# Moving four taps of a depthwise convolution from TensorE to VectorE and ScalarE in a transformer block

## The chip, the core and the metric

The kernel runs on one core of one Trainium2 chip. The time of a run is the device time of that core in microseconds (us). Five engines have instruction queues of their own: TensorE (PE in the profile, its weight loads PEld), VectorE (DVE), ScalarE (ACT), GpSimd (POOL) and SyncE (SP), which here only issues DMAs. Each runs its queue strictly in order, and semaphores order them against each other.

## The reference

One block, 256 tokens of width 1024: attention with eight heads beside a depthwise convolution, a projection, and a gated feed-forward part. Cut to what matters:

```python
u = rms_norm(h, mix_norm_g)
q, k, v, glu_a, glu_g = split(u @ w_in)            # 5 x 512 columns
attn_out = attention(heads(q), heads(k), heads(v), rel_bias)
# convolution, 512 channels, 31 causal taps for each channel
c = glu_a * sigmoid(glu_g)
c = depthwise_conv(c, conv_w) + conv_b
c = (c - mean(c)) * rsqrt(var(c) + 1e-5) * conv_ln_g + conv_ln_b
conv_out = silu(c)
h = h + concat(attn_out, conv_out) @ w_out
u = rms_norm(h, ffn_norm_g)
h = h + (silu(u @ w_gate) * (u @ w_up)) @ w_down   # width 2816
out = rms_norm(h, final_norm_g)
```

With 256 tokens there is one attention block, so it is plain causal softmax attention with a bias by distance.

## The kernel before

All data are float32. A product of two matrices is made of three: each operand is split into an upper part, rounded to the format that TensorE takes in one pass (`wh`, `uh`), and a lower part, the rest (`wl`, `ul`); the products are wh x uh, wh x ul, wl x uh. ScalarE makes a weight's upper part by a copy (step `h`), VectorE the lower part by a subtraction (step `w`, which also makes the upper part if `h` has not). Weights come in pairs of 512 KB tiles from HBM into six raw buffers (step `ld`, on SP's queue); a buffer comes free when its lower part has been made. SP issues in program order, and each load waits for the semaphore of the one eight places before it.

The order of the first part is written out by hand. `PROGRAM` is a table of steps; `ops` maps each name to a function and they are called in that order, so each engine's queue is the order of the table cut to its own instructions. The names that matter here:

- `a0.k`, `a1.i`: projection to the two halves of glu_a and glu_g; half 0 and half 1 are 256 channels each, in two chunks of 128. `sq`: squares of x on ScalarE, summed on VectorE in `accx`. `rs`: `rstd`, the scaling of the first norm: two matmuls `ps_x`, VectorE's `ms_x`, GpSimd's power `rc_x`, VectorE's two diagonals `dg_x`. `rb`: a matmul `pb_x` with the diagonals spreads the scaling over all partitions.
- `glu.half`: sigmoid and products into `upad`, padded by 30 columns. `ud`, `us`: `upad` goes through HBM into `ustk`, where one partition block of 32 holds one of four shifts.
- `cw.half` (`conv_weights`): VectorE makes `wstk`, the diagonal blocks of the convolution's weights, 32 columns for each of 48 instructions, out of `pv`. `pv` holds small columns; the late ones (taps, weights, an identity) come by `pl`, one DMA of 78 KB on SP's queue.
- `c.half.j` (`conv`): TensorE does four taps at a time, in `Q` = 6 quads: 24 taps, 24 matmuls of 128 x 32 by 256 for each chunk, into `pc`. `ct.half.lo.hi` (`conv_taps`): VectorE does the `ONV` = 7 others, one instruction for a tap and chunk, added up in `cacc`; tap 0 is a `tensor_scalar` with the bias. `co.half`: adds `pc` to `cacc`.
- `qk`, `qo`, `sc`, `t`, `n`, `fl`, `fo`: for a pair of heads hp, q and k, their scaling by `rb`, scores, logits and exponentials, division by the sum (`normed`), transposes, copies. `v`, `vt`, `pv`, `mo`: values, their scaling, the product with the probabilities, and the split of the result into `mh` and `ml`.
- `l.1` to `l.7` (`norm`): the convolution's norm over channels: mean by a matmul `pm` (2), subtraction, squares (6), sums (3), `rstd` (7), the matmul `pb_ln` (4), and in 5 the scaling of `cacc`, Silu, and the split into `mh` and `ml`, for four chunks. `o.k`: projection w_out for one chunk k of eight; `f.m`: its last three chunks for output block m, and the sum with x.

Behind the table comes the feed-forward part: eleven groups, each of gate and up products (`pf`) and the down product (`pd`) of an earlier group, then the last norm. There a third call of `rstd` also made two diagonals, which nothing reads.

[...]

Of the kernel before, what the change touches and what calls it, by code (L numbers as in the profile page):

```python
# [23 lines left out]
CC = 4  # L24
# [16 lines left out]
MIX = 48  # L41

PROGRAM = """
ld.a1_0 a0.0 a0.1 a0.2 a0.3 ld.a1_1 a0.4 a0.5 a0.6 hb pz a0.7 pl ld.qk0
w.a1_0.0 w.a1_0.1 zs zd sq.0 sq.1 w.a1_0.2 w.a1_0.3 sq.2 sq.3 sq.4 ld.qk1 a1.0 w.a1_1.0 sq.5 sq.6 sq.7 h.a1_1.1 h.qk0.0 h.qk0.1 a1.1 rs
w.a1_1.1 w.qk0.0 bd ld.qk2 a1.2 rb glu.0 ud.0 w.qk0.1 ld.v0 us.0 a1.3 w.qk1.0 w.qk1.1 glu.1 ud.1 ld.qk3 us.1
qk.0.0 qk.0.1 qo.0 h.qk2.0 h.qk2.1 w.qk2.0 w.qk2.1 cw.0 qk.1.0 ct.0.0.1 ld.v1 qk.1.1 qo.1 h.v0.0 h.v0.1 ct.0.1.3 qk.2.0 sc.0 sc.1 t.0 t.1
c.0.0 ct.0.3.4 h.qk3.0 w.v0.0 n.0 n.1 c.0.1 w.v0.1 h.qk3.1 w.qk3.0 ct.0.4.5 ct.0.5.7 qk.2.1 qo.2 ld.o0 fl.0 fo.0 fl.1 fo.1 w.qk3.1 co.0 h.v1.0 cw.1 w.v1.0
v.0 ld.o1 qk.3.0 h.v1.1 w.v1.1 h.o0.0 ct.1.0.2 qk.3.1 qo.3 h.o0.1 w.o0.0 ct.1.2.3 v.1 sc.2 sc.3 t.2 t.3 ld.o2
c.1.0 ct.1.3.4 n.2 n.3 c.1.1 ct.1.4.6 ct.1.6.7 h.o1.0 co.1 l.1 v.2 w.o0.1 v.3 fl.2 fl.3 vt fo.2 fo.3 l.2 ld.o3 w.o1.0  # L50
pv.0 mo.0 pv.1 mo.1 l.6 pv.2 mo.2 pv.3 mo.3 l.3 w.o1.1 ld.g0 w.o2.0 w.o2.1 ld.u0 o.0 o.1 l.7 w.o3.0 o.2 w.o3.1 ld.g1 l.4 l.5 w.g0.0 o.3 w.g0.1 o.4
# [10 lines left out]
def block_kernel(ctx, tc, xT, w_in, w_out, w_gu, w_down, pvec, gfin, relb, hot, out):  # L62
# [24 lines left out]
    act, vec, pool, sync = (InOrder(e) for e in (nc.scalar, nc.vector, nc.gpsimd, nc.sync))  # L87
# [92 lines left out]
    us = const.tile([P, KD * 2 * S + SHIFT], F32R, name="us")  # L180
# [3 lines left out]
    pv = const.tile([P, PV_N + 8], F32, name="pv")  # L184
# [3 lines left out]
    warm = const.tile([P, 1], F32, name="warm")  # L188
    accx = w1.tile([P, S], F32, name="accx")
# [5 lines left out]
    wstk = [w1.tile([P, 8 * Q, 32], F32, name=f"wstk{i}", tag="wstk", bufs=2) for i in range(2)]  # L195
# [23 lines left out]
    zs = w1.tile([H, ZN], F32, name="zs", tag="lg", bufs=2)  # L219
# [5 lines left out]
    col = lambda lo, i: pv[:, lo + i : lo + i + 1]  # L225


    def conv_weights(half):
        fold, cw = pv[:, PV_FOLD:PV_N], pv[:, PV_CW + half * 8 * Q :]
        vec.tensor_tensor(  # L230
            wstk[half],
            bass.AP(tensor=fold.tensor, offset=fold.offset, ap=[fold.ap[0], [0, 8 * Q], [1, 32]]),
            bass.AP(tensor=cw.tensor, offset=cw.offset, ap=[cw.ap[0], [1, 8 * Q], [0, 32]]), op=ALU.mult)

    def rstd(acc, n, eps, name, b):
        ps = bank(b, f"ps_{name}")
        for t in range(2):
            mm(ps[:, t : t + 1], acc[:, t * P : (t + 1) * P], ones[:, 0:1], start=True, stop=True)  # L240
# [310 lines left out]
    def a0(k):  # L551
# [284 lines left out]
```

## Time and profile before

| | us |
|---|---|
| median of 3 runs (294.02 to 294.55) | 294.12 |
| the profiled execution | 294.47 |
| its span, first to last instruction | 292.6 |
| TensorE busy in the span | 285.2 (97%) |
| VectorE | 201.9 (69%) |
| ScalarE | 151.7 (52%) |
| GpSimd | 42.8 (15%) |

The granted TensorE clock is 0.995 of full speed in the mean. A busy TensorE is not TensorE at its peak: the ends of its matmuls are modelled, and they overlap, so the distance from start to start is what counts. In the timelines, rows of the same form in a row are merged, with their number behind an x, and the duration is from the first start to the last end. An idle time in brackets is that of the engine just before the row, with what ended it.

### The profile page before, as it was taken

How to read it: one execution, taken by the hardware profiler on the slowest of the kernel's cores; microseconds unless marked ns; L12 is line 12 of the kernel's file. 1: busy time of each engine (PE TensorE's matmuls, PEld its weight loads, DVE VectorE, ACT ScalarE, POOL GpSimd, SP SyncE). 2: the span in 40 equal slices, each digit the busy share in tenths (PEclk: the TensorE clock that was granted, in tenths of full speed). 3: DMA queues.
4: the chain of work that ended last, by engine and by line, in shares of the span. 5: the costliest groups of instructions: out<-in, count | busy, mean ns of one | idle time of the engine just before them, and what ended most of it. 6: DMA issues, size and time to landing. Idle time of an engine off the chain costs nothing.

```text
span 292.6 us, 4768 instructions
## 1 busy us (share of the span) xinstructions
PE 285.2 (97%) x1749; PEld 244.7 (84%) x1749; DVE 201.9 (69%) x371; ACT 151.7 (52%) x260; POOL 42.8 (15%) x80
## 2 busy tenths in 40 slices
PE   8999999999999999999999999999999999999991
PEld 8999996986899998888888888888888888888881
DVE  3987999988897788967937557381738366321884
ACT  3885548908393678537717263361718173402531
POOL 2000100000000000143121313321401313130000
PEclk9999999999999999999999999999999999999998
DMA  7999699951138435999996949879794949420012
GB/s 216 339 391 335 239 292 240 386 163 63 66 95 283 156 123 202 272 329 290 355 273 170 305 129 325 300 227 369 239 281 155 299 120 328 143 72 0 0 59 87
DMA packets 22090, 63.74 MB, mean 218 GB/s; under 512 B 3178, under 2 KB 5938, under 8 KB 22066
## 3 DMA queue, kind: packets, MB, share of 16 engines
q1 hardware_dynamic: 18754, 54.94, 56.8%
q0 software_dynamic: 2880, 7.95, 10.1%
q10 hardware_dynamic: 432, 0.54, 0.5%
q8 instruction: 14, 0.23, 0.3%
q14 instruction: 10, 0.08, 0.1%
HBM read 58.10 MB, written 5.32 MB: 217 GB/s over the span
## 4 chain that ended last, share of the span: by engine, by line
PE 92%; issue 2%; DVE 2%; DMA 1%; SPq 1%; ACT 0%; POOLq 0%; POOL 0%; DVEq 0%
PE pf L74 41%; PE pd L74 18%; PE py L74 8%; PE pqk L74 8%; PE pv L74 4%; PE pc L74 4%; PE pa L74 3%; PE pg L74 3%; DMA raw_a<-in_w_in 1%; PE pt L77 1%; PE ps L74 1%; PE po L74 1%; DVE ht L85 1%; SPq L85 1%; DVE hg L85 0%
## 5 line engine op out<-in xcount | busy, mean ns | idle before, releaser
L74 PE MATMUL pf<-wl,us 128*128 128x512 f32 x176 | 68.5, 389 | 0.0
L74 PE MATMUL pf<-wh_u,us 128*128 128x512 f32 x176 | 56.3, 390 | 0.0
L74 PE MATMUL pf<-wh_g,us 128*128 128x512 f32 x176 | 56.0, 389 | 0.0
L85 DVE TENSOR_TENSOR ff<-fs,pf 128x256 f32<-128x256 f32 x22 | 9.1, 419 | 53.9 <-ACT fs L85 53.9
L85 ACT ACTIVATE fs<-pf,rc_h 128x256 f32<-128x256 f32 x22 | 10.4, 475 | 67.2 <-PE pf L74 66.7
L74 PEld LDWEIGHTS pf<-wh_u,us 128*128 128x128 f32 x176 | 33.1, 188 | 6.9
L74 PEld LDWEIGHTS pf<-wh_g,us 128*128 128x128 f32 x176 | 33.0, 188 | 6.9
L74 PEld LDWEIGHTS pf<-wl,us 128*128 128x128 f32 x176 | 33.0, 188 | 6.7
L74 PE MATMUL pd<-wh_d,fh 128*128 128x512 f32 x84 | 32.9, 391 | 0.0
L74 PE MATMUL pd<-wh_d,fl 128*128 128x512 f32 x84 | 32.7, 390 | 0.0
L74 PE MATMUL pd<-wl,fh 128*128 128x512 f32 x84 | 32.7, 389 | 0.0
L85 DVE TENSOR_TENSOR wl<-raw_u,wh_u 128x1024 fp32r<-128x1024 f32 x22 | 26.4, 1221 | 7.9 <-ACT wh_u L85 7.9
L85 ACT CAST wh_u<-raw_u 128x1024 fp32r<-128x1024 f32 x22 | 22.8, 1053 | 13.5 <-PE pf L74 10.2
L85 POOL DMA_DIRECT2D fb<-fd x40 | 23.2, 587 | 43.7 <-issue 24.6
L85 DVE TENSOR_TENSOR wl<-raw_g,wh_g 128x1024 fp32r<-128x1024 f32 x22 | 25.9, 1218 | 1.5 <-ACT wh_g L85 1.5
L85 DVE TENSOR_TENSOR wl<-raw_d,wh_d 128x1024 fp32r<-128x1024 f32 x22 | 25.6, 1204 | 0.5 <-ACT wh_d L85 0.5
L74 PE MATMUL pqk<-us,wh_qk 128*128 128x256 f32 x128 | 22.2, 278 | 0.0
L85 ACT CAST wh_g<-raw_g 128x1024 fp32r<-128x1024 f32 x22 | 22.0, 1048 | 0.0
L85 ACT CAST wh_d<-raw_d 128x1024 fp32r<-128x1024 f32 x22 | 21.9, 1047 | 0.0
L74 PEld LDWEIGHTS pqk<-us,wh_qk 128*128 128x128 f32 x128 | 19.4, 188 | 0.5 <-issue 0.4
L74 PEld LDWEIGHTS pd<-wh_d,fl 128*128 128x128 f32 x84 | 15.8, 188 | 3.3
L74 PEld LDWEIGHTS pd<-wh_d,fh 128*128 128x128 f32 x84 | 15.8, 188 | 3.2
(155 smaller groups left out, 527.4 us busy)
## 6 DMA issues: line engine op xcount, KB each, us to landing
raw_g<-in_w_gu SPq DMA_DIRECT2D x22, 512.0 KB, 5.2
raw_u<-in_w_gu SPq DMA_DIRECT2D x22, 512.0 KB, 6.1
raw_d<-in_w_down SPq DMA_DIRECT2D x22, 512.0 KB, 4.3
raw_qk<-in_w_in SPq DMA_DIRECT2D x8, 512.0 KB, 7.3
raw_o<-in_w_out SPq DMA_DIRECT2D x8, 512.0 KB, 4.1
raw_a<-in_w_in SPq DMA_DIRECT2D x12, 256.0 KB, 4.3
fd<-fv POOLq DMA_DIRECT2D x10, 256.0 KB, 3.9
fb<-fd POOLq DMA_DIRECT2D x40, 64.0 KB, 4.9
```

The lines of the kernel that those rows point to most:

```text
L74: return tc.keep_in_program_order(nc.tensor.matmul(*args, **kw))
L77: return tc.keep_in_program_order(nc.tensor.transpose(o, i, ident))
L85: return lambda *a, **k: tc.keep_in_program_order(f(*a, **k))
```

## The change

`Q` goes from 6 to 5: TensorE does 20 taps, 80 instructions of the convolution in place of 96, and `ONV` becomes 11. Tap 0 of each chunk, with the bias, goes to ScalarE (step `ca`); VectorE does ten taps for each chunk, 40 instructions where it had 24 and four `tensor_scalar`. The blocks of `wstk` are made in four pieces of 640 columns (steps `cw.half.j`) where two of 1536 stood; those of half 0 are made much earlier, and `pl` goes ahead of the load of a1_1 for that. `rstd` no longer makes the diagonals; `diagonal` does, called for two of its three uses. All divisions of the softmax go to ScalarE. The Silu table is drawn in `mix_out(3)`. The lower part of o3.1 goes behind `l.5`.

```diff
-Q = 6
+Q = 5
 ONV = TAPS - 4 * Q
...
-ld.a1_0 a0.0 a0.1 a0.2 a0.3 ld.a1_1 a0.4 a0.5 a0.6 hb pz a0.7 pl ld.qk0
+ld.a1_0 a0.0 a0.1 a0.2 a0.3 pl ld.a1_1 a0.4 a0.5 a0.6 hb pz a0.7 ld.qk0
...
-    def conv_weights(half):
-        fold, cw = pv[:, PV_FOLD:PV_N], pv[:, PV_CW + half * 8 * Q :]
+    def conv_weights(half, j):
+        n = 4 * Q
+        fold, cw = pv[:, PV_FOLD:PV_N], pv[:, PV_CW + (2 * half + j) * n :]
         vec.tensor_tensor(
-            wstk[half],
+            wstk[half][:, j * n : j * n + n],
...
         pool.tensor_tensor(rc, ms, mhalf[:, 0:2], op=ALU.pow)
+        return rc
+
+    def diagonal(rc, name):
         dg = const.tile([P, S], F32, name=f"dg_{name}", tag="dg")
         for t in range(2):
             vec.tensor_scalar(dg[:, t * P : (t + 1) * P], ident, rc[:, t : t + 1], None, op0=ALU.mult)
-        return rc, dg
+        return dg
...
         if n == 0:
-            vec.tensor_scalar(cv(c), u, w, col(PV_CB, c), op0=ALU.mult, op1=ALU.add)
+            act.activation(cv(c), u, AF.Identity, scale=w, bias=col(PV_CB, c))
...
-        if hp == 3:
-            act.activation(warm, sm[:, 3, 1, 1:2], AF.Silu)
...
-                p, r = prb[hp, e][:, cols], rs[:, hp, e, t : t + 1]
-                if hp < 2:
-                    act.activation(p, p, AF.Copy, scale=r)
-                else:
-                    vec.tensor_scalar(p, p, r, None, op0=ALU.mult)
+                p = prb[hp, e][:, cols]
+                act.activation(p, p, AF.Copy, scale=rs[:, hp, e, t : t + 1])
...
         act.copy(mh[:, hp], po[hp][:, 0:S])
+        if hp == 3:
+            act.activation(warm, sm[:, 3, 1, 1:2], AF.Silu)
...
-            rc2, _ = rstd(acch, D, RMS_EPS, "h", next(spare))
+            rc2 = rstd(acch, D, RMS_EPS, "h", next(spare))
```

What the table does to VectorE's queue shows at three places. In these rows L85 is the helper that records every instruction, out<-in are the tiles, then the size. The first place is from the lower parts of a1_0 (`wl` from `raw_a_0`) to the first norm's scaling. VectorE before:

```order
L85 TENSOR_TENSOR wl<-raw_a_0_1_152,wh_a_0_1_305 128x512 x2
L85 TENSOR_TENSOR accx<-accx,sq_x_320 128x256
L85 TENSOR_TENSOR accx<-accx,sq_x_323 128x256
L85 TENSOR_TENSOR accx<-accx,sq_x_326 128x256
L85 TENSOR_TENSOR wl<-raw_a_1_0_223,wh_a_1_0_357 128x1024
L85 TENSOR_TENSOR accx<-accx,sq_x_361 128x256
L85 TENSOR_TENSOR accx<-accx,sq_x_364 128x256
L85 TENSOR_TENSOR accx<-accx,sq_x_367 128x256
L85 TENSOR_SCALAR ms_x<-ps_x 128x2
```

The two lower parts stand in one row, and `ms_x` directly behind the sums of squares. VectorE in the changed kernel, same place:

```order
L85 TENSOR_TENSOR wl<-raw_a_0_1_152,wh_a_0_1_305 128x512
L85 TENSOR_TENSOR wstk_83<-pv 128x640
L85 TENSOR_TENSOR wl<-raw_a_0_1_152,wh_a_0_1_305 128x512
L85 TENSOR_TENSOR accx<-accx,sq_x_321 128x256
L85 TENSOR_TENSOR accx<-accx,sq_x_324 128x256
L85 TENSOR_TENSOR accx<-accx,sq_x_327 128x256
L85 TENSOR_TENSOR wl<-raw_a_1_0_224,wh_a_1_0_358 128x1024
L85 TENSOR_TENSOR accx<-accx,sq_x_362 128x256
L85 TENSOR_TENSOR accx<-accx,sq_x_365 128x256
L85 TENSOR_TENSOR accx<-accx,sq_x_368 128x256
L85 TENSOR_TENSOR wstk_83<-pv 128x640
L85 TENSOR_SCALAR ms_x<-ps_x 128x2
```

The two pieces of half 0's blocks now stand there, the first between the last two lower parts of a1_0 and the second between the sums of squares and `ms_x`.

The second place is the end of the convolution's half 1 beside the second two heads' divisions. VectorE before, from the third reciprocal on:

```order
L85 RECIPROCAL rs<-sm 128x2
L85 TENSOR_SCALAR p_964<-p_964,rs 128x128
L85 TENSOR_SCALAR p_964<-p_964,rs 128x256
L85 RECIPROCAL rs<-sm 128x2
L85 TENSOR_SCALAR p_971<-p_971,rs 128x128
L85 TENSOR_SCALAR p_971<-p_971,rs 128x256
L85 SCALAR_TENSOR_TENSOR cacc<-upad_82,pv,cacc 128x256 x6
L85 TENSOR_TENSOR cacc<-pc_979,cacc 128x256 x2
L85 TENSOR_TENSOR s_149<-cacc 128x256
L85 TENSOR_TENSOR s_149<-s_149 128x256
L85 TENSOR_TENSOR wl<-raw_o_1_806,wh_o_1_886 128x1024
```

Two taps, two reciprocals and four divisions of the same kind stand ahead of these rows, behind the logits. VectorE in the changed kernel, from the taps behind the logits on:

```order
L85 SCALAR_TENSOR_TENSOR cacc<-upad_82,pv,cacc 128x256 x4
L85 RECIPROCAL rs<-sm 128x2 x4
L85 SCALAR_TENSOR_TENSOR cacc<-upad_82,pv,cacc 128x256 x8
L85 TENSOR_TENSOR cacc<-pc_984,cacc 128x256 x2
L85 TENSOR_TENSOR s_149<-cacc 128x256
L85 TENSOR_TENSOR s_149<-s_149 128x256
L85 TENSOR_SCALAR vt<-pv_843,rc_x 128x512
L85 TENSOR_TENSOR wl<-raw_o_1_807,wh_o_1_888 128x1024
```

The divisions have gone from here, twelve tap instructions stand behind the logits where eight stood, and the scaling of the values (`vt`) goes ahead of a lower part.

The third place is the convolution's norm from its scaling on. VectorE before:

```order
L85 TENSOR_SCALAR ms_ln<-ps_ln 128x2
L85 TENSOR_SCALAR dg_ln<-ident,rc_ln 128x128 x2
L85 TENSOR_TENSOR wl<-raw_o_0_1110,wh_o_0_1231 128x1024
L85 TENSOR_TENSOR wl<-raw_o_1_1111,wh_o_1_1232 128x1024
L85 TENSOR_TENSOR cacc<-cacc,pb_ln 128x256 x4
L85 TENSOR_TENSOR ml<-csq,mh 128x256 x4
L85 TENSOR_TENSOR wl<-raw_g_0_1155,wh_g_0_1283 128x1024
```

Both lower parts of o3 stand between the diagonals and the scaling by `pb_ln`. VectorE in the changed kernel, same place:

```order
L85 TENSOR_SCALAR ms_ln<-ps_ln 128x2
L85 TENSOR_SCALAR dg_ln<-ident,rc_ln 128x128 x2
L85 TENSOR_TENSOR wl<-raw_o_0_1111,wh_o_0_1233 128x1024
L85 TENSOR_TENSOR cacc<-cacc,pb_ln 128x256 x4
L85 TENSOR_TENSOR ml<-csq,mh 128x256 x4
L85 TENSOR_TENSOR wl<-raw_o_1_1112,wh_o_1_1234 128x1024
L85 TENSOR_TENSOR wl<-raw_g_0_1157,wh_g_0_1285 128x1024
```

One of the two lower parts that stood ahead of the scaling by `pb_ln` now stands behind the four `ml`.

## Rows read from the trace of the kernel before

**Rows 1.** Chain of waits in order of time: start us, us, what, records.

```profile
44.86 5.32 PE pc L74 x96
...
67.00 5.32 PE pc L74 x96
...
275.27 2.79 PE pd L74 x12
```

**Rows 2.** VectorE timeline, 39 to 80 us: start, us, operation, records, [idle before, releaser].

```profile
39.13 1.75 DVE L85 TENSOR_TENSOR wstk<-pv 128x1536 f32<-128x1536 f32 x1
...
51.47 2.46 DVE L85 SCALAR_TENSOR_TENSOR cacc<-upad,pv,cacc 128x256 f32<-128x256 f32 x6
...
62.76 0.69 DVE L85 TENSOR_TENSOR qk<-pqk,rb 128x512 f32<-128x512 f32 x1 [0.60 <-PE pqk L74]
...
66.38 0.29 DVE L85 CUSTOM_DVE_ANT_0 lg<-ps,bias 128x128 f32<-128x128 f32 x1 [0.99 <-PE ps L74]
...
69.23 0.88 DVE L85 SCALAR_TENSOR_TENSOR cacc<-upad,pv,cacc 128x256 f32<-128x256 f32 x2
```

**Rows 3.** VectorE timeline, 12 to 50 us.

```profile
18.22 0.69 DVE L85 TENSOR_TENSOR wl<-raw_a,wh_a 128x512 fp32r<-128x512 f32 x1 [0.53 <-ACT wh_a L85]
...
21.37 1.47 DVE L85 TENSOR_TENSOR accx<-accx,sq_x 128x256 f32<-128x256 f32 x3
23.67 0.16 DVE L85 TENSOR_SCALAR ms_x<-ps_x 128x2 f32<-128x2 f32 x1 [0.83 <-PE ps_x L74]
...
29.75 3.49 DVE L85 TENSOR_TENSOR wl<-raw_qk,wh_qk 128x1024 fp32r<-128x1024 f32 x3
```

**Rows 4.** DMA issues by tile, 0 to 40 us: engine, count, KB, us to landing.

```profile
raw_a<-in_w_in SPq DMA_DIRECT2D x2, 512.0 KB, 6.8
...
pv<-in_pvec SPq DMA_DIRECT2D x1, 78.0 KB, 7.1
```

**Rows 5.** ScalarE timeline, 12 to 50 us.

```profile
17.57 0.62 ACT L85 CAST wh_a<-raw_a 128x512 fp32r<-128x512 f32 x1 [0.78 <-DMA raw_a<-in_w_in]
```

**Rows 6.** Stretches: us, each engine's busy time (records), PEclk, DMA share, GB/s.

```profile
16.00:30.00 14.00, 14.00 (x121) 13.82 (x121) 11.17 (x24) 9.72 (x18) 1.43 (x2) 1.00 1.00 368
```

**Rows 7.** TensorE timeline, 16 to 40 us.

```profile
23.13 0.50 PE L74 MATMUL ps_x<-ones,accx 128*128 128x1 f32 x4
...
31.08 0.34 PE L74 MATMUL pqk<-us,wl 128*128 128x256 f32 x1
```

**Rows 8.** TensorE timeline, 78 to 100 us.

```profile
79.19 0.60 PE L74 MATMUL pm<-s,invc 128*128 128x256 f32 x2
...
91.44 0.59 PE L74 MATMUL pb_ln<-dg_ln,ones 128*128 128x256 f32 x2
...
98.24 0.28 PE L74 MATMUL py<-mh,wl 128*128 128x256 f32 x1
```

**Rows 9.** ScalarE timeline, 50 to 95 us.

```profile
49.51 2.58 ACT L85 ACTIVATE p<-p,rs 128x256 f32<-128x256 f32 x7
...
70.41 1.28 ACT L85 ACT_TABLE_LOAD   x1
71.70 0.20 ACT L85 ACTIVATE warm<-sm 128x1 f32<-128x1 f32 x1
...
83.32 4.86 ACT L85 CAST wh_o<-raw_o 128x1024 fp32r<-128x1024 f32 x5
```

**Rows 10.** VectorE timeline, 78 to 98 us.

```profile
79.83 1.41 DVE L85 TENSOR_TENSOR cacc<-cacc,pm 128x256 f32<-128x256 f32 x4 [0.99 <-PE pm L74]
...
88.79 0.16 DVE L85 TENSOR_SCALAR ms_ln<-ps_ln 128x2 f32<-128x2 f32 x1 [0.31 <-PE ps_ln L74]
89.80 0.48 DVE L85 TENSOR_SCALAR dg_ln<-ident,rc_ln 128x128 f32<-128x128 f32 x2 [0.85 <-POOL rc_ln L85]
...
92.46 1.41 DVE L85 TENSOR_TENSOR cacc<-cacc,pb_ln 128x256 f32<-128x256 f32 x4
...
96.87 0.43 DVE L85 TENSOR_TENSOR ml<-csq,mh 128x256 fp32r<-128x256 f32 x1 [0.51 <-ACT mh L85]
```

More of the change, by code (lines that the diff above doesn't have):

```diff
@@ L43 @@
 PROGRAM = """
-ld.a1_0 a0.0 a0.1 a0.2 a0.3 ld.a1_1 a0.4 a0.5 a0.6 hb pz a0.7 pl ld.qk0
[L45 to L51, printed above, removed]
+ld.a1_0 a0.0 a0.1 a0.2 a0.3 pl ld.a1_1 a0.4 a0.5 a0.6 hb pz a0.7 ld.qk0
+w.a1_0.0 w.a1_0.1 zs zd sq.0 sq.1 w.a1_0.2 cw.0.1 w.a1_0.3 sq.2 sq.3 sq.4 ld.qk1 a1.0 w.a1_1.0 sq.5 sq.6 sq.7 h.a1_1.1 h.qk0.0 h.qk0.1 a1.1 cw.0.0 rs rd
+w.a1_1.1 w.qk0.0 bd ld.qk2 a1.2 rb glu.0 ud.0 w.qk0.1 ld.v0 us.0 a1.3 w.qk1.0 w.qk1.1 ca.0 glu.1 ud.1 ld.qk3 us.1
+qk.0.0 qk.0.1 qo.0 h.qk2.0 h.qk2.1 ca.1 w.qk2.0 w.qk2.1 ct.0.1.3 qk.1.0 ct.0.3.4 ld.v1 qk.1.1 qo.1 h.v0.0 h.v0.1 ct.0.4.6 qk.2.0 sc.0 sc.1 t.0 t.1
+c.0.0 ct.0.6.7 h.qk3.0 w.v0.0 n.0 n.1 c.0.1 w.v0.1 h.qk3.1 w.qk3.0 ct.0.7.8 ct.0.8.10 qk.2.1 qo.2 ld.o0 fl.0 fo.0 fl.1 fo.1 w.qk3.1 h.v1.0 ct.0.10.11 co.0 w.v1.0
+v.0 ld.o1 qk.3.0 h.v1.1 w.v1.1 h.o0.0 ct.1.1.3 qk.3.1 qo.3 h.o0.1 w.o0.0 cw.1.0 cw.1.1 ct.1.3.5 v.1 sc.2 sc.3 t.2 t.3 ld.o2
+c.1.0 ct.1.5.7 n.2 n.3 c.1.1 ct.1.7.9 ct.1.9.11 h.o1.0 co.1 l.1 v.2 v.3 fl.2 fl.3 vt w.o0.1 fo.2 fo.3 l.2 ld.o3 w.o1.0
+pv.0 mo.0 pv.1 mo.1 l.6 pv.2 mo.2 pv.3 mo.3 l.3 w.o1.1 ld.g0 w.o2.0 w.o2.1 ld.u0 o.0 o.1 l.7 w.o3.0 o.2 h.o3.1 ld.g1 l.4 l.5 w.o3.1 w.g0.0 o.3 w.g0.1 o.4
 f.0 f.1 g.0 f.2 g.1 f.3 g.2 f.4 g.3 f.5 g.4 f.6 g.5 f.7 g.6 g.7 w.u0.0 ld.u1 w.u0.1 ld.g2 hs.0 hs.1 hs.2 hs.3 hs.4 hs.5 hs.6 hs.7 w.g1.0 w.g1.1
@@ L225, in block_kernel @@
     col = lambda lo, i: pv[:, lo + i : lo + i + 1]
-    def conv_weights(half):
-        fold, cw = pv[:, PV_FOLD:PV_N], pv[:, PV_CW + half * 8 * Q :]
+    def conv_weights(half, j):
+        n = 4 * Q
+        fold, cw = pv[:, PV_FOLD:PV_N], pv[:, PV_CW + (2 * half + j) * n :]
         vec.tensor_tensor(
-            wstk[half],
-            bass.AP(tensor=fold.tensor, offset=fold.offset, ap=[fold.ap[0], [0, 8 * Q], [1, 32]]),
-            bass.AP(tensor=cw.tensor, offset=cw.offset, ap=[cw.ap[0], [1, 8 * Q], [0, 32]]), op=ALU.mult)
+            wstk[half][:, j * n : j * n + n],
+            bass.AP(tensor=fold.tensor, offset=fold.offset, ap=[fold.ap[0], [0, n], [1, 32]]),
+            bass.AP(tensor=cw.tensor, offset=cw.offset, ap=[cw.ap[0], [1, n], [0, 32]]), op=ALU.mult)
     def rstd(acc, n, eps, name, b):
@@ L350, in scale_x, with scale_diagonal @@
     def scale_x():
-        xn["c"], xn["d"] = rstd(accx, D, RMS_EPS, "x", 5)
+        xn["c"] = rstd(accx, D, RMS_EPS, "x", 5)
+    def scale_diagonal():
+        xn["d"] = diagonal(xn["c"], "x")
     rb = w1.tile([P, S], F32, name="rb")
@@ L527, in norm @@
         elif part == 7:
-            _, ln["dg"] = rstd(s4[:, 0], CC * P, LN_EPS, "ln", 4)
+            ln["dg"] = diagonal(rstd(s4[:, 0], CC * P, LN_EPS, "ln", 4), "ln")
         elif part == 4:
@@ L556, in a0 @@
         a_mm(0, k, f"a0_{k // 4 * 4}", k % 4 * 512)
-    ops = {"ld": fetch, "zd": bias_out, "bd": bias_in, "ud": stack_out, "us": stack_in, "h": high, "w": split, "rb": row_scale, "hb": bias_parts, "pl": late_columns, "pz": bias_mm, "zs": bias_copy, "vt": v_out, "rs": scale_x,
+    ops = {"ld": fetch, "zd": bias_out, "bd": bias_in, "ud": stack_out, "us": stack_in, "h": high, "w": split, "rb": row_scale, "hb": bias_parts, "pl": late_columns, "pz": bias_mm, "zs": bias_copy, "vt": v_out, "rs": scale_x, "rd": scale_diagonal, "ca": lambda half: conv_taps(half, 0, 1),
            "a0": a0, "a1": a1, "glu": glu, "qk": qk_mm, "qo": qk_out, "sc": score, "t": logits, "n": normed, "fl": flip,
```

## The prediction

> **What bounds the kernel now.** I read the chain of waits first, in order of time. From about 9 us to 278.06 us it is TensorE alone: each piece begins where the one before it ended; the two convolutions and the last piece stand in [rows 1]. So in this stretch a matmul that goes away is worth its step on TensorE, and work of VectorE and ScalarE costs nothing until a matmul waits for it. Their timelines then say where that can happen: the reader is to look for places with no slack between a lower part or a scaling and the matmul that takes it.
>
> The profiled execution took 294.47 us (span 292.6 and 1.9 around it); the median of three runs is 294.12. I sum against 294.47 and take the difference off the median.
>
> **TensorE: 32 records fewer.** One half of the convolution is 48 instructions, which leave 96 records (two for each float32 matmul) in 5.32 us [rows 1]: 55.4 ns each. With five quads it is 40 instructions, 80 records: 16 x 55.4 ns = 0.89 us less, and there are two halves: **-1.77 us**. Nothing hides this, since the pieces before and after are TensorE's own. Behind the first half TensorE runs 0.89 earlier, behind the second 1.77, and so does all that waits for it; the feed-forward part and its loads follow TensorE as a whole.
>
> **VectorE's early gaps, and the load that moved.** The blocks of half 0 are made in two pieces of 640 columns. The piece of 1536 lasted 1.75 us [rows 2] and a lower part of 512 columns 0.69 [rows 3]; on the line between them 640 columns last 0.82. Queued work starts about 0.08 before the one ahead ends (six taps of 0.48 take 2.46, 0.40 a step [rows 2]), so a piece costs 0.74. The first goes into the 0.53 us in which VectorE waited for ScalarE before 18.22 [rows 3], 0.61 with the overlap: 0.13 too long. It also waits for the late columns of pv, whose DMA now stands ahead of the two 512 KB loads of a1_1 on SP's queue. When do they land? Before, they took 7.1 us from issue to landing, and the two loads ahead of them 6.8 [rows 4]; 78 KB took as long as 512, so this was the queue. Now what is ahead of them is the last piece of a1_0, for which ScalarE waited until 17.57 [rows 5]. At the 368 GB/s of that stretch [rows 6] 78 KB is 0.21 us, so I put the landing at 17.77 and VectorE's wait L, which would start at 17.62, at 0.15, with 0 and 0.7 as bounds. The loads of a1_1 land 0.2 later, which ScalarE's squares ahead of their casts cover.
>
> The second piece goes into the 0.83 us before 23.67 [rows 3] (0.91 with the overlap) and wins back 0.17. VectorE is then 0.13 + L - 0.17 = L - 0.04 late, 0.11 for L = 0.15. Queued behind it are the scaling ms_x, with GpSimd's power and the diagonals waiting for that, then the glu, and then the lower part of qk0.1, which began at 29.75 and ended at 30.97, the first of three at 1.14 a step [rows 3]. The matmul that takes it began at 31.08 and lasted 0.34 [rows 7], where its neighbours of the same form last 0.28: TensorE already waited 0.06. There is no slack, so TensorE gets the delay in full: **+0.11 us** (bounds 0 and 0.7). The sums of squares, ended at 22.84 [rows 3], come 0.28 late against some 0.2 of slack to ps_x at 23.13 [rows 7]; those 0.1 are part of the same delay, not a second one.
>
> **VectorE from 39 to 80 us.** Half 0: out go a piece of 1.67 a step and two first taps of 0.33; in come eight taps of 0.40. Six of these precede the first logits, which about evens out, and the logits waited for TensorE's scores. Half 1 is the tight one. VectorE waited 0.60 us for TensorE before 62.76 [rows 2]; that now comes at 62.76 + 0.11 - 0.89 = 61.98, and the work ahead of it has become 0.73 shorter (1.67 and 0.65 out, four taps in). Then, in steps: scaling of q and k 0.61, lower part 1.13, two pieces 1.48, four taps 1.59: logits at 66.8, 66.38 before [rows 2]. The convolution wants the first piece at 67.00 - 0.78 = 66.2 [rows 1]; it is there at 64.5. Logits 2.85 (66.38 to 69.23 [rows 2]), four taps 1.59, reciprocals 0.26, eight taps 3.17, sums 1.58: done at 76.25. TensorE wants the sum at pm, 79.19 - 1.66 = 77.5 [rows 8]: 1.3 us to spare. The divisions are eight activations on ScalarE, seven of which took 2.58 [rows 9]: 71.3 to 74.2. Their transposes come 1.3 before pm, at 76.2: 2 to spare. Tap 0 stands on ScalarE where it waited for VectorE. Cost 0 while these covers last.
>
> **The table load and the norm.** The Silu load leaves the place behind the exponentials and stands ahead of the five casts of w_out that began at 83.32. It lasts 1.28, and the activation behind it starts 1.29 after it [rows 9]. The first cast then ends at 83.32 - 1.66 + 1.29 + 0.10 + 1.04 = 84.1. VectorE waited 0.31 before ms_ln at 88.79 [rows 10], so it had begun the three lower parts ahead of it at 88.48 - 3.42 = 85.06, now 83.4: it waits 0.7 there, ms_ln is 0.4 late, and the diagonals, which ended at 90.28 for pb_ln at 91.44 [rows 8, 10], keep 0.8 of their 1.16. Cost 0. [...]
>
> The scaling by pb_ln no longer stands behind the lower part of o3.1, and that stands behind the norm's four ml. In times of before: pb_ln at 91.44, its reader 0.64 later (as pm at 79.19 and its reader at 79.83), 4.41 to the last ml (92.46 to 96.87), 0.35 for that and 1.22 for the lower part: 98.06 [rows 8, 10]. TensorE takes it at 98.24 [rows 8], and loads it somewhat before. That is between 0 and 0.2 us; I take **+0.05**, as the row leans to the free side. The norm's own earlier end gives nothing, as TensorE waited for none of it.
>
> **Sum.** -1.77 + 0.11 + 0.05 = **-1.6 us**: 292.9 for the profiled execution, **292.5** for the median. A measurement of this kernel can tell about 0.2%, 0.6 us, from no change, so 293.5 divides faster from same.
>
> **Rivals.**
> - *VectorE becomes the bound ahead of pm.* If in that dense stretch a tap cost its duration, 0.48, and not its step, the twenty of half 1 would take 1.6 more and pm wait 0.3, with as much again behind it. For it: hardly an idle place is left there. Against: queued taps before show 0.40 [rows 2]. It gives back 0.3 to 0.8: about 293.1. Chance 0.13.
> - *The table load holds ScalarE for longer than its row.* pb_ln waits once it is 0.8 longer; at twice its 1.28 it waits 0.5: 293.0. Before, at 70.41, the next activation came with no such gap [rows 9]: 0.04. [...]
> - *The late columns keep their 7.1 us.* If it is their DMA that is slow (rows of 624 bytes) and not the queue, an issue at about 12.1 gives 19.2, L = 1.6, TensorE 1.56 late: -0.2, 294.0, no change. Against it, 6.8 for the large loads [rows 4]. Chance 0.10.
> - *Slower: the late columns land only where they landed, at 20.4.* L = 2.8; the last lower part of a1_0 and the sums of squares are queued behind the piece, and ps_x and all behind it get 2.76: +1.0, 295.2. It turns from gain to loss at a landing of 19.4 and is beyond measurement from 20.0. It needs the place in the queue not to matter. Chance 0.07.
>
> The forecast has 0.66. The range goes from 292.1 (no delay at all, and 0.2 of spread) to 293.6 (L at 0.7 with the lower part's 0.2, and the first two rivals); it leaves out the last two rivals, 0.17. Faster 0.83, same 0.10, slower 0.07.
>
> **What would show each step.** Two pc pieces of 80 records in 4.43 us each; TensorE's pieces without gaps from 9 to 276 us. VectorE's first row of 640 columns at 17.6 to 18.3; ms_x within 0.2 of 23.67; the row of 31.08 about 0.1 later. The sum done near 76.3 and pm near 77.5; the transposes without a wait. The casts of w_out right behind the table load, near 83; pb_ln without a wait; the row of 98.24 near 96.6 and no longer than 0.28. I am wrong if TensorE shows an idle place, or a matmul much longer than its neighbours, at ps_x, pm, pb_ln or the first output block.

## The result

The changed kernel takes **292.93 us** (median of 5 runs, 292.65 to 293.02); the kernel before takes 294.43 beside it (5 runs, 294.02 to 294.60). The ratio is 0.995, 95% interval 0.994 to 0.9961: 1.50 us less, where 1.6 was forecast. The 292.5 forecast for the median itself was 0.4 too low, of which 0.3 is the kernel before, whose median was 294.12 when the forecast was made. A second series of the changed kernel gave 292.90 against 294.38 (0.9944, 0.9932 to 0.9956). The profiled execution has a span of 291.1 us, 1.5 below that of before.

The chain of waits of the changed kernel (start us, us, what, records) still is TensorE alone:

```profile
9.22 0.74 PE pa L74 x4
...
13.40 0.68 PE pa L74 x6
...
29.74 13.76 PE pqk L74 x120
...
45.01 4.45 PE pc L74 x80
...
66.27 4.45 PE pc L74 x80
...
77.77 0.43 PE pm L74 x2
...
90.05 0.43 PE pb_ln L74 x2
```

The two convolution pieces answer to [rows 1]: 80 records in 4.45 us each for 96 in 5.32, so 0.87 less twice. Before, TensorE's stretch began at 9.13 us and that of qk was 13.69 long: 0.09 and 0.07 have come in there.

VectorE's timeline of the changed kernel (start, us, operation, records, [idle before, releaser]), the places of [rows 2, 3 and 10]:

```profile
17.71 0.81 DVE L85 TENSOR_TENSOR wstk<-pv 128x640 f32<-128x640 f32 x1
...
22.96 0.82 DVE L85 TENSOR_TENSOR wstk<-pv 128x640 f32<-128x640 f32 x1
23.75 0.16 DVE L85 TENSOR_SCALAR ms_x<-ps_x 128x2 f32<-128x2 f32 x1
...
29.92 3.49 DVE L85 TENSOR_TENSOR wl<-raw_qk,wh_qk 128x1024 fp32r<-128x1024 f32 x3
...
44.38 0.29 DVE L85 CUSTOM_DVE_ANT_0 lg<-ps,bias 128x128 f32<-128x128 f32 x1 [0.44 <-PE ps L74]
...
66.83 0.28 DVE L85 CUSTOM_DVE_ANT_0 lg<-ps,bias 128x128 f32<-128x128 f32 x1
...
71.26 0.35 DVE L85 RECIPROCAL rs<-sm 128x2 f32<-128x2 f32 x4
71.52 3.24 DVE L85 SCALAR_TENSOR_TENSOR cacc<-upad,pv,cacc 128x256 f32<-128x256 f32 x8
...
75.92 0.42 DVE L85 TENSOR_TENSOR s<-s 128x256 f32<-128x256 f32 x1
...
84.33 3.50 DVE L85 TENSOR_TENSOR wl<-raw_o,wh_o 128x1024 fp32r<-128x1024 f32 x3 [0.85 <-ACT wh_o L85]
87.74 0.15 DVE L85 TENSOR_SCALAR ms_ln<-ps_ln 128x2 f32<-128x2 f32 x1
...
95.28 1.22 DVE L85 TENSOR_TENSOR wl<-raw_o,wh_o 128x1024 fp32r<-128x1024 f32 x1
```

ScalarE's timeline, for [rows 9]; the DMA issue that answers to the last line of [rows 4] (KB, us to landing); and four rows of TensorE's timeline, for [rows 7 and 8] and the products po:

```profile
71.51 2.88 ACT L85 ACTIVATE p<-p,rs 128x128 f32<-128x128 f32 x8 [0.68 <-DVE rs L85]
...
81.86 1.28 ACT L85 ACT_TABLE_LOAD   x1
83.15 0.20 ACT L85 ACTIVATE warm<-sm 128x1 f32<-128x1 f32 x1
83.26 4.84 ACT L85 CAST wh_o<-raw_o 128x1024 fp32r<-128x1024 f32 x5
```

```profile
pv<-in_pvec SPq DMA_DIRECT2D x1, 78.0 KB, 4.7
```

```profile
31.19 0.39 PE L74 MATMUL pqk<-us,wl 128*128 128x256 f32 x1
...
77.60 0.60 PE L74 MATMUL pm<-s,invc 128*128 128x256 f32 x2
78.13 2.82 PE L74 MATMUL po<-pts,vt 128*64 128x256 f32 x32
...
96.69 0.28 PE L74 MATMUL py<-mh,wl 128*128 128x256 f32 x1
```

What to see: three of the four idle brackets of [rows 2 and 3] are gone (0.53 before the lower part, 0.83 before ms_x, 0.99 before the logits at 66.38); the fourth, 0.60 before the scaling of q and k, is still 0.45. No new one stands on TensorE. One matmul is longer than its neighbours: 0.39 at 31.19, where the one before the change had 0.34 and the others 0.28.

### The profile page after: what moved, and what is told of

It reads as the page before. It is cut to its first block, busy times and chain, and to the rows that moved or that the text cites. A ratio compares the mean times of both kernels' runs of the same rounds, so it can differ in the third digit from the quotient of the medians.

```text
span 291.1 us, 4726 instructions
## 1 busy us (share of the span) xinstructions
PE 283.6 (97%) x1717; PEld 243.4 (84%) x1717; DVE 203.6 (70%) x375; ACT 156.7 (54%) x272; POOL 43.6 (15%) x80
## 3 DMA queue, kind: packets, MB, share of 16 engines
HBM read 58.10 MB, written 5.32 MB: 218 GB/s over the span
## 4 chain that ended last, share of the span: by engine, by line
PE 92%; issue 2%; DVE 2%; DMA 2%; SPq 1%; ACT 1%; POOLq 0%; POOL 0%; DVEq 0%
PE pf L74 41%; PE pd L74 18%; PE py L74 8%; PE pqk L74 8%; PE pv L74 4%; PE pa L74 3%; PE pg L74 3%; PE pc L74 3%; DMA raw_a<-in_w_in 2%; PE pt L77 1%; PE ps L74 1%; PE po L74 1%; DVE ht L85 1%; SPq L85 1%; DVE hg L85 0%
## 5 line engine op out<-in xcount | busy, mean ns | idle before, releaser
L85 DVE TENSOR_TENSOR ff<-fs,pf 128x256 f32<-128x256 f32 x22 | 9.1, 419 | 55.4 <-ACT fs L85 55.4
L85 ACT ACTIVATE fs<-pf,rc_h 128x256 f32<-128x256 f32 x22 | 10.3, 475 | 67.3 <-PE pf L74 65.8
L85 DVE TENSOR_TENSOR wl<-raw_u,wh_u 128x1024 fp32r<-128x1024 f32 x22 | 26.5, 1220 | 8.7 <-ACT wh_u L85 8.7
L85 ACT CAST wh_u<-raw_u 128x1024 fp32r<-128x1024 f32 x22 | 22.8, 1051 | 14.6 <-PE pf L74 10.9
L85 POOL DMA_DIRECT2D fb<-fd x40 | 23.2, 585 | 45.1 <-issue 23.5
L85 DVE TENSOR_TENSOR wl<-raw_g,wh_g 128x1024 fp32r<-128x1024 f32 x22 | 25.9, 1217 | 1.0 <-ACT wh_g L85 1.0
L85 DVE TENSOR_TENSOR wl<-raw_d,wh_d 128x1024 fp32r<-128x1024 f32 x22 | 25.6, 1202 | 0.5 <-ACT wh_d L85 0.5
L85 ACT CAST wh_g<-raw_g 128x1024 fp32r<-128x1024 f32 x22 | 22.0, 1049 | 0.0
L85 ACT CAST wh_d<-raw_d 128x1024 fp32r<-128x1024 f32 x22 | 21.9, 1047 | 0.0
L74 PEld LDWEIGHTS pd<-wl,fh 128*128 128x128 f32 x84 | 15.8, 188 | 3.2
```

The costliest lines, as they stand in the source:

```text
L74: return tc.keep_in_program_order(nc.tensor.matmul(*args, **kw))
L85: return lambda *a, **k: tc.keep_in_program_order(f(*a, **k))
```

## The experiments

The question behind them: are TensorE's 32 records the whole gain, and which of the other parts does that gain need? Differences below are medians against the kernel before in the same series, whose median lay between 294.31 and 294.46. TensorE's start differs by some tenths between executions, with the landing of the first loads: in six profiles its stretch begins at 8.91 to 9.28 us, 2.22 to 2.24 behind the landing of a first load at 6.68 to 7.04. So what is smaller than 0.3 us is read from waits in the trace, not from the times.

**Six quads back, everything else kept**

```
-Q = 5
+Q = 6          # taps cut to the seven that are left
```

> The changed kernel with six quads put back on TensorE and seven taps on VectorE and ScalarE; all other parts of the change stay. Theory A (the gain is TensorE's 32 records alone, the other parts only keep VectorE and ScalarE out of its way): the gain of 1.5 us goes, both convolution pieces are 96 records in 5.32 us again, and the two early pieces of blocks, 768 columns and so 0.13 us longer each, put a stall of 0.1 to 0.3 us on the lower part that had none to spare: +0.2 to +0.5 us against the kernel before. Theory B (the earlier norm scaling, the divisions on ScalarE and the table load's new place bring time of their own): -0.3 us or better.

Measured: +0.56 us (294.95, 12 runs; ratio 1.0018, 1.001 to 1.0027). Both pc pieces are 96 records in 5.32 us again. The loss beyond the gain is at the early pieces, in VectorE's and TensorE's timelines:

```profile
17.87 0.96 DVE L85 TENSOR_TENSOR wstk<-pv 128x768 f32<-128x768 f32 x1 [0.24 <-DMA pv<-in_pvec]
```

```profile
23.42 0.61 PE L74 MATMUL ps_x<-ones,accx 128*128 128x1 f32 x4 [0.19 <-DVE accx L85]
```

Theory A, with a loss just beyond its +0.5: without the records nothing of the gain is left. In this execution the late columns landed 0.24 us after VectorE wanted them, and ps_x waited.

**Five quads alone, in the kernel before**

```
-... ct.0.4.5 ct.0.5.7 ...     -... ct.1.4.6 ct.1.6.7 ...
+... ct.0.4.5 ct.0.5.11 ...    +... ct.1.4.6 ct.1.6.11 ...
```

> The kernel before with five quads instead of six and the four further taps of each half behind its last ones on VectorE; nothing else of the change. Theory A: TensorE's convolution pieces shrink to 4.45 us each, but 3.17 us of taps stand in each half with no place made for them. VectorE comes some 3 us late to the scaling of q and k near 62.8 us and to the sums, which end near 81 where pm would want them at 77.5: TensorE waits 3 to 4 us in all, so +0.5 to +2.5 us against the kernel before. Theory B (VectorE has the room anyway): -1.3 to -1.8 us, TensorE without gaps.

Measured: +3.93 us (298.32, 4 runs; ratio 1.0127, 1.0109 to 1.0144), beyond either expectation. TensorE's waits (for whom, us, times, longest), two stretches of 2 us (each engine's busy time, then the granted clock, DMA share, GB/s), and a row of TensorE's timeline:

```profile
PE pm L74 <- DVE s L85: 2.3, 1, 2.3
...
PE pqk L74 <- DVE wl L85: 0.9, 1, 0.9
...
PE po L74 <- DVE vt L85: 0.5, 1, 0.5
```

```profile
82.00:84.00 2.00, 1.55 (x12) 0.90 (x12) 2.00 (x6) 0.31 (x1) 0.00 (x0) 0.69 0.36 70
84.00:86.00 2.00, 2.00 (x18) 1.43 (x15) 2.00 (x4) 1.09 (x5) 0.00 (x0) 0.50 0.51 197
```

```profile
82.95 3.96 PE L74 MATMUL po<-pts,vt 128*64 128x128 f32 x28 [0.45 <-DVE vt L85]
```

The waits are 3.7 us, inside the 3 to 4 that Theory A had summed. What it lacked is behind them: the granted clock fell from 1.00 to 0.50 (84 to 86 us). Of the 32 records of po, 28 stand behind the last wait; the next product starts 3.89 us after the first of them (82.95 to 86.84), and 2.27 in the changed kernel (78.61 to 80.88). So the clock cost 1.6 us. With -1.74 for the records that makes 3.6 of the 4.2 us by which this execution's span is the longer one; the rest lies in the steps around the waits. So the record count is worth 1.74 only if the taps have places; without them the change is a loss.

**The eight divisions back on VectorE**

```
-                act.activation(p, p, AF.Copy, scale=rs[:, hp, e, t : t + 1])
...
+                if hp < 2:
+                    act.activation(p, p, AF.Copy, scale=r)
+                else:
+                    vec.tensor_scalar(p, p, r, None, op0=ALU.mult)
```

> The changed kernel with the eight divisions of the second two pairs of heads back on VectorE. Theory A (they bring no time of their own, they keep VectorE free for the taps): 8 instructions at 0.23 us a step put 1.8 us more ahead of the sums, which end near 78.2 us where pm wants them at 77.6, and VectorE's half of the scaling vt, queued behind them, ends near 79.0 where the products of po want it near 78.4: TensorE waits 0.6 to 1.2 us, so -0.9 to -0.3 us against the kernel before, and up to 1.2 more if the granted clock falls behind the wait as it did with the four further taps alone. Theory B (VectorE has the 1.8 us to spare): -1.6 to -1.4.

Measured: +0.34 us (294.80, 11 runs; ratio 1.0016, 1.0007 to 1.0024). TensorE's waits, and VectorE's timeline:

```profile
PE pm L74 <- DVE s L85: 1.1, 1, 1.1
...
PE py L74 <- DVE ml L85: 0.8, 1, 0.8
```

```profile
71.07 0.16 DVE L85 RECIPROCAL rs<-sm 128x2 f32<-128x2 f32 x1
...
73.70 3.25 DVE L85 SCALAR_TENSOR_TENSOR cacc<-upad,pv,cacc 128x256 f32<-128x256 f32 x8
```

Theory A's place was right and its size was short. The sums ended at 78.53 for 78.2, pm waited 1.1, and what VectorE was still behind by came out at the first output block, which no expectation had named: its second operand ml was 0.8 late. The size was short because the expectation took 8 x 0.23 = 1.8 us: from the first reciprocal to the eight taps there are 2.63 us, and 0.26 in the changed kernel, so the divisions cost VectorE 2.37. Less the 1.26 us that the sums had to spare ahead of pm, that is the 1.1 at pm. The two waits make 1.9 us. No fall of the granted clock shows: it was 0.997 in the mean, as in the changed kernel, and the 32 records of po between the waits took 2.82 us in both.

**The lower part of o3.1 back ahead of the norm's scaling**

```
-... o.2 h.o3.1 ld.g1 l.4 l.5 w.o3.1 w.g0.0 ...
+... o.2 w.o3.1 ld.g1 l.4 l.5 w.g0.0 ...
```

> The changed kernel with the lower part of o3.1 (cast and subtraction) back ahead of the norm's scaling. Theory A, from the profile of the changed kernel: VectorE begins the scaling by pb_ln 1.1 us later, the norm's four outputs come about 1.0 later, and the last of them misses the output projection's matmul on it by 0 to 0.4 us: -1.5 to -1.1 us against the kernel before, with a wait of TensorE at the last ml if any. Theory B (the scaling ahead of the lower part is worth its whole 1.1 us): -0.5 to -0.3. If it is worth nothing at all: -1.6 to -1.5.

Measured: -1.26 us (293.13, 5 runs; ratio 0.9961, 0.9948 to 0.9973). In VectorE's and TensorE's timelines:

```profile
92.85 0.43 DVE L85 TENSOR_TENSOR ml<-csq,mh 128x256 fp32r<-128x256 f32 x1 [0.17 <-ACT mh L85]
```

```profile
92.93 0.32 PE L74 MATMUL py<-mh,wh_o 128*128 128x256 f32 x1
93.33 0.39 PE L74 MATMUL py<-ml,wh_o 128*128 128x256 f32 x1
```

The first of the norm's ml ends at 93.28 and the matmul that takes it starts at 93.33, 0.28 later than its neighbours' step of 0.11 to 0.12 allows; the one behind it is another 0.1 late. From the first output block to the first product of the feed-forward part TensorE takes 23.48 us, and 23.06 in the changed kernel. So the part keeps away about 0.4 us. In the kernel before, with the same order, the first ml ended at 94.48, and its matmul ran in step at 94.72. The difference is not TensorE's earlier arrival alone: ms_ln now starts 1.03 us behind ps_ln, 0.54 before, since VectorE waits for casts that stand behind the table load; no run tells the two apart. It was the first ml that missed, and not the last as the expectation had it.

**The late columns back behind the loads of a1_1, twice**

```
-... a0.3 pl ld.a1_1 a0.4 a0.5 a0.6 hb pz a0.7 ld.qk0
+... a0.3 ld.a1_1 a0.4 a0.5 a0.6 hb pz a0.7 pl ld.qk0
```

> The changed kernel with the DMA of the late columns of pv back behind the two loads of a1_1 on SP's queue. Theory A (its landing is set by its place in the queue; the piece of blocks queued ahead of the last lower part of a1_0 waits for it): landing at about 20.2 to 20.4 us, VectorE idle 2.4 to 2.7 us ahead of the first piece of 640 columns, TensorE waits 2.3 to 2.7 at ps_x or behind it, and the kernel is 0.8 to 1.2 us slower than before. Theory B (the place in the queue doesn't matter, as the load itself takes its time): -1.5, like the changed kernel. Theory C (VectorE's wait is made good further on): between the two, -1.0 to 0.

Measured: +2.47 us (296.86, 6 runs from 294.95 to 297.86; ratio 1.0076, 1.0048 to 1.0103). The profiled execution was the fastest: columns at 19.8 us, VectorE idle 2.66 us, ps_x 2.47 late. That is Theory A's mechanism, and by its time, 294.95, this execution is 0.6 us slower than the kernel before. The median is 1.9 more, so the kernel ran once more.

> The changed kernel with the DMA of pv's late columns behind the two loads of a1_1, once more, since its first profile (span 293.2 us, 2.1 above the changed kernel, columns landed at 19.8) was its fastest execution, and its median was 2.0 us above that. Theory A (the columns land later in most executions): a landing after 20.5 us, VectorE idle one for one longer ahead of the piece of blocks, TensorE's wait at ps_x as much longer, granted clock 1.00 behind it. Theory B (the landing is about the same, but the granted clock falls behind TensorE's wait): landing at 19.5 to 20.5, and a stretch between 22 and 32 us with a granted clock below 0.9.

Measured: +3.10 us (297.41, 4 runs; ratio 1.0119, 1.0081 to 1.0156), 295.97 in the profiled one. TensorE's wait at ps_x, then stretches of 2 us as above:

```profile
24.73 0.61 PE L74 MATMUL ps_x<-ones,accx 128*128 128x1 f32 x4 [1.56 <-DVE accx L85]
```

```profile
26.00:28.00 2.00, 2.00 (x14) 2.00 (x13) 1.61 (x3) 0.00 (x0) 0.35 (x1) 0.60 1.08 371
28.00:30.00 2.00, 2.00 (x11) 1.93 (x10) 1.23 (x2) 0.00 (x0) 0.00 (x0) 0.55 0.94 293
```

Theory B's mechanism: the wait is shorter than in the first profile, 1.56 for 2.47, and the columns were taken at 19.3, yet the execution is a microsecond longer, because the granted clock fell to 0.60 and 0.55 in the stretches from 26 to 30 us, where the first execution kept 1.00. Six matmuls that take 0.68 us at a granted clock of 1.00 took 1.28. A wait that hit TensorE cost itself alone in one execution and itself plus 1.6 us in another (from ps_x to the start of the qk stretch 8.27 us, 6.65 in the first profile). Why 2.47 us of waiting left the clock at 1.00 and 1.56 brought it to 0.55 stays open.

The profile is of the fastest execution in both series. The record has the mean granted clock of the others: in the first series 0.995 at 295.68 us, and 0.990 to 0.992 in the four from 296.76 to 297.86; in the second 0.992 at 297.31 and 297.51, as in the profiled one, and 0.985 at 298.67. So the slower clock goes with the long executions. It is not all of it: two of the second series are 1.3 and 1.5 us longer than the profiled one at the same mean clock, and what adds that, a later landing perhaps, is not shown.

**The table load back behind the exponentials**

```
+        if hp == 3:                                               # in logits
+            act.activation(warm, sm[:, 3, 1, 1:2], AF.Silu)
...
-        if hp == 3:                                               # in mix_out
-            act.activation(warm, sm[:, 3, 1, 1:2], AF.Silu)
```

> The changed kernel with the Silu table load back behind the exponentials of the last pair of heads. Theory A (a load costs its row of 1.28 us and is covered in either place): divisions, cast, vt and the copies of pts on ScalarE come 0.5 to 1.2 us later and still ahead of po; the casts of w_out begin 1.3 earlier; -1.6 to -1.3 us against the kernel before, as the changed kernel. Theory B (the new place is part of the gain): -0.6 or worse, with TensorE waiting at the transposes or at po. [...]

Measured: -1.39 us (293.07, 5 runs; ratio 0.9949, 0.9936 to 0.9961): the changed kernel's time. From the start of the qk stretch to that of the first output block TensorE takes 51.25 us, and 51.21 in the changed kernel. The row ACT_TABLE_LOAD lasts 1.28 us in both places, with the tiny activation `warm` 1.29 behind its start (71.72 and 73.01; 81.86 and 83.15 in the changed kernel). The load is covered in both; its move buys nothing.

**The lower part of qk0.1 ahead of the glu**

```
-... rb glu.0 ud.0 w.qk0.1 ld.v0 us.0 ...
+... rb w.qk0.1 glu.0 ud.0 ld.v0 us.0 ...
```

> The changed kernel with the lower part of qk0.1 made ahead of the first half's glu, not behind it. Theory A (VectorE's 0.1 us at the second piece of blocks reaches TensorE through that lower part and nothing else): the row near 31.19 us lasts 0.28 instead of 0.39, the stretch of qk is 13.65 instead of 13.76 us, and the kernel is 0.1 faster than the changed one: -1.7 to -1.5 us against the kernel before. Theory B (the 0.1 us comes from elsewhere, or the glu made 1.1 us later is itself late, for the transfers of the shifted rows or for the activation of tap 0): the long row stays or another appears, -1.4 or worse.

Measured: -1.46 us (293.00, 9 runs; ratio 0.9955, 0.994 to 0.997). The long matmul is gone, all near 31 us last 0.28, so Theory A names the right place. But the transfers of the shifted rows are now issued 1.9 us later, and in the profiled execution, the longest of the nine (294.67; the others end at 293.39), the convolution waited for them:

```profile
PE pc L74 <- DMA ustk<-ud: 1.8, 1, 1.8
```

So Theory B holds too in that execution: 0.1 us won, and a cover lost. Those transfers also took longer there (8.1 us to landing in the median, 6.1 in the changed kernel), so not all of the 1.8 is shown to come from their place. By time the kernel is no better.

**The blocks of half 0 back near 39 us, and then three parts undone together**

```
-... w.a1_0.2 cw.0.1 w.a1_0.3 ... a1.1 cw.0.0 rs rd
+... w.a1_0.2 w.a1_0.3 ... a1.1 rs rd
-... w.qk2.1 ct.0.1.3 ...
+... w.qk2.1 cw.0.0 cw.0.1 ct.0.1.3 ...
```

> The changed kernel with both pieces of blocks of half 0 back behind the lower parts of qk2, near 39 us. Theory A (VectorE's early gaps are free, and near 39 us the 1.5 us of these pieces push the first logits 1.0 us and with them the divisions): the transposes near 52.4 us wait 0.2 to 0.8 us, while the 0.1 us at 31.19 goes: -1.4 to -0.8 us against the kernel before. Theory B (the stretch from 39 to 52 us has room for them): -1.7 to -1.5, as fast as the changed kernel or faster.

Measured: -1.67 us (292.79, 6 runs; ratio 0.9948, 0.9933 to 0.9962). Theory A falls: TensorE did not wait at the transposes; its one wait of the profiled execution was 0.5 us at ps_x, for sums whose loads had come late. Next, the late columns and the table load went back as well:

> The changed kernel without three of its parts: the blocks of half 0 stand behind the lower parts of qk2 near 39 us, the DMA of pv's late columns behind the loads of a1_1, and the Silu table load behind the exponentials, all as in the kernel before. What is left is the five quads with their taps in the new order, the divisions on ScalarE and the norm's scaling ahead of o3.1's lower part. Theory A (only the taps' places and the divisions are needed for the gain): -1.7 to -1.3 us against the kernel before, as the changed kernel. Theory B (each of the three parts covers for another): the transposes near 52.4 us or pm near 77.6 wait: -1.0 or worse.

Measured: -1.71 us (292.67, 5 runs from 292.57 to 292.84; ratio 0.9942, 0.9929 to 0.9954), beside the changed kernel's own second series:

> The changed kernel itself once more, beside the kernels of this round. By every theory -1.5 us against the kernel before (-1.8 to -1.2), with 0.2 to 0.5 us of spread from when the first loads land.

That gave -1.48 (292.90, 292.29 to 293.16); the two intervals overlap, so the shorter version is as good and cannot be called better. VectorE's timeline of it:

```profile
38.91 1.55 DVE L85 TENSOR_TENSOR wstk<-pv 128x640 f32<-128x640 f32 x2
...
44.94 0.29 DVE L85 CUSTOM_DVE_ANT_0 lg<-ps,bias 128x128 f32<-128x128 f32 x1
```

Theory A. The logits come with no idle time before them, where the changed kernel has 0.44 for the scores; TensorE waits for nothing behind its first matmuls. The 1.5 us of pieces take up that idle time and more, and nothing behind them came too late. Their early place, the early transfer that it needs, and the table load's move are thus not part of the gain. Of what is left, the runs price the records, the divisions and o3.1's place one by one; no run puts tap 0 back on VectorE, or the scaling of the values back behind the lower part.

**Four quads in half 1, the four taps on GpSimd**

```
+                pool.tensor_scalar(m, u, col(PV_T, n * CC + c), None, op0=ALU.mult)
+                pool.tensor_tensor(cv(c), cv(c), m, op=ALU.add)
```

> The changed kernel with four quads in the second half of the convolution; its four further taps are made by GpSimd, as 8 multiplications and 8 additions of 128x256 right behind tap 0, in the stretch from 39 us in which GpSimd has nothing to do. Theory A (TensorE's records are the gain, as long as the taps find an engine that nobody waits for): the second convolution piece is 64 records in 3.56 us, the sums end near 76.3 us where pm now wants them at 76.7, no wait: 0.9 less than the changed kernel, -2.5 to -2.2 us against the kernel before. Theory B (work of GpSimd slows VectorE's instructions beside it, or takes so long that VectorE's first tap of the half, near 60 us, waits for it): the taps and lower parts from 39 to 60 us last longer in the trace, TensorE waits at the transposes near 52 or at pm, -1.6 or worse.

Measured: +2.06 us (296.44, 5 runs; ratio 1.0064, 1.0052 to 1.0076). VectorE's and GpSimd's timelines, and a piece of TensorE's chain:

```profile
39.50 3.87 DVE L86 SCALAR_TENSOR_TENSOR cacc<-upad,pv,cacc 128x256 f32<-128x256 f32 x6
43.29 0.68 DVE L86 TENSOR_TENSOR qk<-pqk,rb 128x512 f32<-128x512 f32 x1
...
52.29 1.76 DVE L86 TENSOR_TENSOR wl<-raw_qk,wh_qk 128x1024 fp32r<-128x1024 f32 x1
```

```profile
49.85 1.89 POOL L86 TENSOR_SCALAR pt_m<-upad,pv 128x256 f32<-128x256 f32 x1
51.82 1.14 POOL L86 TENSOR_TENSOR cacc<-cacc,pt_m 128x256 f32<-128x256 f32 x1
```

```profile
13.21 0.71 PE pa L75 x6
```

Theory B's mechanism. While GpSimd worked (36.9 to 55.7 us), six taps took 3.87 us, 2.46 without it, and two lower parts 1.76 for 1.22, while a third kept 1.24; GpSimd's own multiplications ran from 0.92 to 1.89. The scaling of q and k, whose input lies in PSUM, kept its 0.68. VectorE arrived late at pm (0.9) and at the first ml (0.8). The engine that nobody waits for was not free.

By time these waits explain only a part. They are 1.7 us against the 0.9 won with the fourth quad, so 0.8 above the changed kernel, and 3.5 was measured. Most of the rest, some 2.6 us over the execution, is in TensorE's steps. The products pa, pg, pqk and pf step slower from the start to the end, at a granted clock of 0.996 in the mean (0.997 in the changed kernel), and pd and py do not: six records of pa take 0.71 us for 0.68 before GpSimd has made a tap, and 48 of pf take 10.99 for 10.88 long after its last one. No other profile shows it, and its cause stays open. So the run shows that GpSimd's work delays VectorE; it does not give the price of this exchange.

## Why the prediction was right, and where its steps were off

- **TensorE's records.** Right: -1.74 for -1.77. Six quads back lose all of it.
- **VectorE's early gaps.** Place and sign right; that the size came out about right is luck. The columns landed 4.7 us after their issue [rows 4 has 7.1], at some 17.4 instead of 17.77, so L was 0 and not 0.15 in this execution. By the text's own L - 0.04 VectorE would then not have been late at all, and at ms_x it was not: ms_x starts 0.53 us behind ps_x, and 0.54 before. The delay comes in behind it. From the first diagonal to the next lower part there are 0.50 us (24.76 to 25.26) where there were 0.40 (24.68 to 25.08). It is 0.49 to 0.50 in the ten profiles with the early pieces and 0.40 in the four without them; what it is stays open. The long matmul at 31.19 came as said, and the qk stretch grew by 0.07 for the 0.11 of the sum. In the execution with six quads L was 0.24, so 0.15 lies inside the spread. The queue was the main cause of the late landing, as taken (last section).
- **VectorE from 39 to 80 us.** Right to a tenth: logits at 66.83 (66.8), sums done at 76.34 (76.25), pm at 77.60 (77.5), divisions 71.51 to 74.39 (71.3 to 74.2). The rival by which a tap costs its duration fell: eight taps took 3.24, 0.40 a step. The spare 1.26 us was as thin as the ledger had it: 2.37 us put back made pm wait for the 1.1 that it did not cover. Where the text closed with "Cost 0 while these covers last" it had no price for their end; the run gives one.
- **The table load.** Right: 1.28 us, and the next activation 1.29 after its start. The first cast let VectorE go at 84.33, idle 0.85 for the 0.7 said, and pb_ln did not wait. The rival by which the load holds ScalarE for longer than its row fell, and the load moved back made no difference (51.25 us from qk to the first output block for 51.21).
- **o3.1.** +0.05 was taken from 0 to 0.2; the lower part ended at 96.50, and the matmul at 96.69 lasted 0.28: 0.
- **The sum.** -1.74 + 0.07 + 0 against the start of TensorE is -1.67; TensorE began 0.09 later by its first loads, which the sum did not have, and some hundredths lie in the output blocks. That makes the -1.5 of the spans.
- **The slower rival.** Its mechanism was shown, its size was short. Its sum has a landing at 19.8 us at +0.4, and the execution with that landing and a full clock is 0.6 slower than the kernel before. But the medians are +2.5 and +3.1, with columns taken at 19.8 and 19.3 in the profiles. The missing term is the clock behind the wait, 1.6 us at po and 1.6 behind ps_x in the two profiles that show it. For the same reason the range's upper end was laid too low for any case in which TensorE stands still; the forecast did not need it.
- **What the text did not ask** is whether each part was needed. It costed the early blocks at +0.11 and looked at the gaps that they fill; that the room near 39 us would also do (0.44 idle before the logits, and shorter pieces than before) could have been worked out from the same rows.

## What to carry to other kernels

When one engine runs without gaps, the gain is the work taken off it, and every other edit is worth only the wait that it keeps away: price each by putting it back in the ledger of the engine that takes the work over, up to the next consumer and the one behind that. An engine that has become tight hands on most of a delay (2.37 us put back ahead of pm, 1.9 of waits), and none of it where what waits for the engine has slack (1.5 us put back near 39 us, no wait). A wait of a busy TensorE can cost its own length and the slower clock behind it (1.56 us and 1.6 more in one execution, 2.47 alone in another).

## What the hardware showed that I had not expected

- The granted clock fell to 0.55 behind a wait of 1.56 us at ps_x and to 0.50 behind waits of 2.3 and 0.5 at pm and po, and stayed at 1.00 behind one of 2.47 at ps_x in another execution of the same kernel. Behind one of 1.8 at pc no fall shows: the 80 records there took 4.52 us for 4.45, and the mean clock was 0.996. The two falls cost 1.6 us each.
- Beside GpSimd's work VectorE's taps took up to 1.6 times as long (six in 3.87 us, 2.46 without it), and two lower parts 1.76 us for 1.22, all with their operands in SBUF; a third lower part kept 1.24, and the scaling of q and k, with one operand in PSUM, its 0.68. GpSimd's own multiplications took 0.92 to 1.89.
- The same 78 KB landed 4.3 to 6.1 us after their issue in the eight profiles with them ahead of the loads of a1_1, and 6.1 to 7.1 us in the five with them behind. The place in SP's queue moves the landing, but the two ranges touch.
